# Partition sums of the key norm and the group norm from two float32r parts

## The chip, the core and the metric

The kernel runs on one core of one Trainium2 chip, in one launch. The metric is the device time of an execution in microseconds (us). A core has a matrix engine (TensorE, PE in the profile, with its weight loads shown as PEld), a vector engine (VectorE, DVE), a scalar engine (ScalarE, ACT), GpSimd (POOL) and SyncE (SP), which issues most transfers. Each runs its own queue of instructions in order, and they wait for each other by semaphores. Products accumulate in PSUM, which ACT and DVE read.

## The reference

Two transformer layers on 256 tokens of width 2048, in float32. The first layer has three branches (a banded attention A, an RWKV-7 time mix B and an attention C over a memory of 256 tokens), the second another three and a feed-forward part. Most of the work is products of the activations with weights. The change lies in branch B, whose 16 heads of 64 are handled here in eight pairs:

```python
def rwkv7_time_mix(...):
    ...
    kk = heads(k * f(k_k))
    kk = kk * lax.rsqrt(jnp.maximum(jnp.sum(kk * kk, axis=-1, keepdims=True), 1e-24))
    k = k * (1.0 + (a - 1.0) * f(k_a))
    ...
    o = rwkv7_scan(rh, dh, kh, vh, -kk, kk * ah)
    mean = jnp.mean(o, axis=-1, keepdims=True)
    var = jnp.mean(jnp.square(o - mean), axis=-1, keepdims=True)
    o = ((o - mean) * lax.rsqrt(var + GN_EPS)).reshape(bsz, s, B_WIDTH) * f(ln_w) + f(ln_b)
    bonus = jnp.sum(rh * kh * f(r_k), axis=-1, keepdims=True) * vh
    return o + bonus.reshape(bsz, s, B_WIDTH)
```

The sum of squares in `kk` is the key norm; `mean` and `var` are the group norm. All three sum over a head's 64 channels.

## The kernel before

Activations are kept with channels on the 128 partitions and the 256 tokens along the free dimension, so a tile of 128x256 holds a pair of heads. A sum over a head's channels is then a sum over partitions; it is made on PE, as a product with the constant `bdones` (two 64x64 blocks of ones on the diagonal, part of the constant tile `con`), and comes out on every partition of the head.

**Products of the weights.** A float32 weight is split into two float32r parts: `wh`, rounded by ACT (line 171), and the rest `wl`, by DVE (line 179) or GpSimd (line 177); the activations lie ready split in `xg`. `gemm_B` (line 182) gives a 128x256 tile by pairs of products, one of 512 columns with `wh` and one of 256 with `wl`; `gemm_A` (line 208) fills two PSUM tiles at once. Their PSUM tiles are named g and come from a pool of three banks (line 117). `evict` (line 218) adds the two halves of a g tile up: ACT copies one to `et`, DVE adds the other.

**Branch B, per pair p.** `rwkv_inputs(p)` (line 528) projects k, r and v. Each projection is evicted into a tile `zr`, of which there are two (line 494), and `shift` (line 429) mixes it with its neighbour token: an ACT multiplication into tile `tA` and a DVE step. Then come the decay, the key norm (lines 557 to 564: square, sum into `pk`, maximum, `rsqrt`, multiplication), the bonus sum and the operands `atrt`, `bt_d`, `kt_d` and `v_d`. `rwkv_inverse(p)` (line 584) inverts a triangular matrix per head and chunk, in five levels of small products (tiles Z and D on PE, Z and tt on DVE). `rwkv_chain(p)` (line 652) goes through four chunks of 64 tokens one after the other (products ch and oT on PE, copies X, U and S on DVE) and ends with the group norm in lines 687 to 698, the chain's tail here. Working tiles of branch B come from `tmp(tag)` (line 523), most with one buffer a tag: a tile takes the buffer over when the last reader of the tile ahead of it in the program is done.

**Order.** The program text issues chain(p), inverse(p + 1), inputs(p + 2) and then fillers: gate projections, products of branch A and merge gates (lines 780 to 823). A scheduler sets each engine's queue from that text by times of its own, within the limits of data and buffers. Two fillers hold PSUM for long: A0 (after the first pair) is copied out into `r16b`, whose memory the keys and values `mkv` of attention C hold until its last head is done, and A1 (after the fifth) overwrites queries that attention A still reads.

Of the kernel before, what the change touches and what calls it, by code (L numbers as in the profile page):

```python
# [100 lines left out]
def _body(tc, a, out):  # L101
    nc = tc.nc
# [26 lines left out]
    def P(n, j=0, w=1):  # L129
        o, _ = _P[n]  # L130
        return par[:, o + j:o + j + w]
# [208 lines left out]
    if True:  # L340
# [182 lines left out]
        def tmp(tag, bufs=1, shape=(128, 256), dt=F32):  # L523
            return rw.tile(list(shape), dt, tag=tag, name=tag, bufs=bufs)

        pair = {}

        def rwkv_inputs(p):

            k = tmp("k")  # L530
            shift(k, raw_tile(gemm_B(a["w1B"][1 + p], xg)), P("mu_k", p), 8 + p)
            r = tmp("r")
            shift(r, raw_tile(gemm_B(a["w1B"][9 + p], xg)), P("mu_r", p), p)
            v = tmp("v")
            shift(v, raw_tile(gemm_B(a["w1B"][17 + p], xg)), P("mu_v", p), 16 + p)
            w2 = tmp("t0")
            nc.sync.dma_start(w2, a["lora2"][p])
            pl = ps_small("pl")
            mm(pl[:, 0:256], w2[:, 0:128], lora)
            mm(pl[:, 256:512], w2[:, 128:256], lora)  # L540
            s = tmp("s")
            nc.scalar.activation(s, pl[:, 0:256], AF.Tanh, bias=hw0[:, p:p + 1], scale=0.5)
            av_ = tmp("a")
            nc.scalar.activation(av_, pl[:, 256:512], AF.Tanh, bias=hw0[:, 8 + p:9 + p], scale=0.5)
            nc.scalar.activation(s, s, AF.Copy, bias=0.5, scale=0.5)
            nc.scalar.activation(av_, av_, AF.Copy, bias=0.5, scale=0.5)
            cum = tmp("cum")
            nc.vector.tensor_tensor_scan(cum, C("scan"), s, 0.0, op0=ALU.mult, op1=ALU.add)
            nc.gpsimd.tensor_sub(s, cum, s)
            e1 = s  # L550
            nc.scalar.activation(e1, s, AF.Exp, scale=-DECAY_C)
            ep = tmp("ep", 2)
            nc.scalar.activation(ep, cum, AF.Exp, scale=-DECAY_C)
            en = cum
            nc.scalar.activation(en, cum, AF.Exp, scale=DECAY_C)

            kk = tmp("kk")
            t0 = tmp("t0")
            nc.scalar.activation(t0, k, AF.Square, scale=P("k_k", p))
            pk = ps_small("pk")  # L560
            mm(pk[:, 0:256], bdones, t0)
            nc.vector.tensor_scalar(t0, pk[:, 0:256], 1e-24, None, op0=ALU.max)
            rsqrt(t0, tmp("tA"))
            nc.vector.scalar_tensor_tensor(kk, k, P("k_k", p), t0, op0=ALU.mult, op1=ALU.mult)

            nc.scalar.activation(t0, av_, AF.Identity, bias=om[:, 25 + p:26 + p], scale=P("k_a", p))
            nc.vector.tensor_mul(k, t0, k)

            nc.vector.scalar_tensor_tensor(t0, r, P("r_k", p), k, op0=ALU.mult, op1=ALU.mult)
            mm(pk[:, 256:512], bdones, t0)  # L570
            nc.vector.tensor_mul(raw[:, 8 + p, :], v, pk[:, 256:512])

            atrt = atrt_b[p % 2]
            diag(atrt, 64, lambda d, sl: nc.vector.scalar_tensor_tensor(
                d, c4(kk)[sl], -1.0, c4(e1)[sl], op0=ALU.mult, op1=ALU.mult))
            nc.vector.tensor_mul(atrt[:, :, 0:64], c4(r), c4(ep))
            nc.gpsimd.tensor_mul(kk, kk, av_)
            diag(bt_d, 0, lambda d, sl: nc.vector.tensor_mul(d, c4(kk)[sl], c4(en)[sl]))
            diag(kt_d, 0, lambda d, sl: nc.vector.tensor_mul(d, c4(k)[sl], c4(en)[sl]))
            diag(v_d, 0, lambda d, sl: nc.gpsimd.tensor_copy(d, c4(v)[sl]))  # L580

            pair[p] = dict(atrt=atrt, ep=ep)
# [69 lines left out]
        def rwkv_chain(p):  # L652

            d = pair.pop(p)
            atrt, ep, tok = d["atrt"], d["ep"], d["tok"]
            po = ps_small("oT", "o")
            S = None
            for c in range(4):
                gm, tf = d["gm"][c // 2][:, c % 2], d["tf"][c // 2][:, c % 2]
                pc = ps_small("ch", "c")  # L660
                if S is not None:
                    mm(pc[:, 0:128], atrt[:, c, 64:192], S, start=True, stop=False)
                mm(pc[:, 0:128], gm[:, 64:192], tok[:, 2, c], start=S is None, stop=True)
                x_ = tmp("X", 1, (128, 128))
                nc.vector.tensor_copy(x_, pc[:, 0:128])
                mm(pc[:, 128:256], tf, x_)
                u_ = tmp("U", 1, (128, 128))
                nc.vector.tensor_copy(u_, pc[:, 128:256])
                if c < 3:
                    mm(pc[:, 256:384], tok[:, 1, c], tok[:, 2, c], start=True, stop=False)  # L670
                    mm(pc[:, 256:384], tok[:, 0, c], u_, start=False, stop=True)
                    sn = tmp("S", 2, (128, 128))
                    dc = ep[:, c * 64 + 63:c * 64 + 64]
                    if S is None:
                        nc.vector.tensor_scalar(sn, pc[:, 256:384], dc, None, op0=ALU.mult)
                    else:
                        sd = tmp("Sd", 1, (128, 128))
                        nc.gpsimd.tensor_scalar(sd, S, dc, None, op0=ALU.mult)
                        nc.vector.scalar_tensor_tensor(sn, pc[:, 256:384], dc, sd, op0=ALU.mult, op1=ALU.add)
                o_ = po[:, c * 64:(c + 1) * 64]  # L680
                if S is not None:
                    mm(o_, S, atrt[:, c, 0:64], start=True, stop=False)
                mm(o_, tok[:, 2, c], gm[:, 0:64], start=S is None, stop=False)
                mm(o_, u_, gm[:, 192:256], start=False, stop=True)
                if c < 3:
                    S = sn
            oT = tmp("oT", 1)
            nc.scalar.copy(oT, po[:, 0:256])

            mm(po[:, 256:512], bdones, oT)  # L690
            nc.vector.scalar_tensor_tensor(oT, po[:, 256:512], -1.0 / 64, oT, op0=ALU.mult, op1=ALU.add)
            q_ = tmp("gq")
            nc.scalar.activation(q_, oT, AF.Square)
            mm(po[:, 0:256], bdones, q_)
            nc.vector.tensor_scalar(q_, po[:, 0:256], 1.0 / 64, GN_EPS, op0=ALU.mult, op1=ALU.add)
            rsqrt(q_, tmp("gy"))
            nc.vector.scalar_tensor_tensor(oT, oT, P("ln_w", p), q_, op0=ALU.mult, op1=ALU.mult)
            nc.vector.scalar_tensor_tensor(raw[:, 8 + p, :], oT, P("ln_b", p), raw[:, 8 + p, :], op0=ALU.add, op1=ALU.add)
# [451 lines left out]
```

## Time and profile before

| | us |
|---|---|
| median of three timed runs | 2940.38 |
| lowest, highest | 2939.12, 2940.76 |
| the profiled execution | 2939.36 |
| its span, first to last instruction | 2937.5 |
| PE, DVE, ACT, GpSimd busy in the span | 2910.8, 1867.4, 1471.0, 573.5 |

The span is 1.86 us shorter than the time of the same execution. Branch B with its fillers runs from about 100 to 880 us; then come the merge, the output product and the second layer. Busy time is the time in which an engine executes instructions; a PE that is busy need not run at its peak, since the ends of its products are modelled. A row of the timeline gives the start, the duration, the engine, the line, the operation, the tile written and those read, how many instructions are merged into it, and in brackets how long the engine had been idle before it and what ended the wait. All products show line 150 or 153, those of the helpers `tr` and `mm`, so they are told apart by their tiles.

### The profile page before, as it was taken

The numbers are of one execution on the slowest core, as the hardware profiler recorded it, in microseconds if no ns is written. First come the engines' busy times: TensorE is split into PE (matmuls) and PEld (weight loads), VectorE is DVE, ScalarE is ACT, GpSimd is POOL, SyncE is SP. The second block draws the span as 40 slices with busy tenths as digits, with TensorE's granted clock in tenths as the row PEclk, the third lists the DMA queues.
The fourth block names the chain that finished last, engine by engine and source line by source line (L and its number), as shares of the span: only waits on it lengthen the run. The fifth ranks groups of instructions, "written<-read, shape, count | busy, mean of one in ns | idle before, by whom it ended". The sixth has DMA issues, their size and how long they took to land.

```text
span 2937.5 us, 44420 instructions
## 1 busy us (share of the span) xinstructions
PE 2910.8 (99%) x16696; PEld 2562.2 (87%) x16696; DVE 1867.4 (64%) x3040; ACT 1471.0 (50%) x2249; POOL 573.5 (20%) x806
## 2 busy tenths in 40 slices
PE   9999999999999999999999999999999999999998
PEld 7888888888988888888888888888888888888887
DVE  7455675567647655657667766666666666666554
ACT  7544455455456554545544454444555444444443
POOL 0676576566652000000000000000000000000000
PEclk9999999999999999999999999999999999999999
DMA  7554344444357555655455555555555555555654
GB/s 287 188 168 131 118 134 138 135 135 133 127 173 239 195 188 197 209 177 174 148 173 172 188 192 188 192 187 193 187 187 194 187 193 188 192 188 189 191 187 150
DMA packets 150535, 522.44 MB, mean 178 GB/s; under 512 B 17120, under 2 KB 22624, under 8 KB 150320
## 3 DMA queue, kind: packets, MB, share of 16 engines
q1 hardware_dynamic: 148064, 513.61, 53.2%
q0 software_dynamic: 1824, 4.98, 0.5%
q8 instruction: 131, 2.15, 0.3%
q10 hardware_dynamic: 432, 1.02, 0.1%
q14 instruction: 84, 0.69, 0.1%
HBM read 514.56 MB, written 4.98 MB: 177 GB/s over the span
## 4 chain that ended last, share of the span: by engine, by line
PE 95%; DVE 3%; ACT 1%; POOL 1%; issue 0%; DMA 0%; DVEq 0%; SPq 0%; ACTq 0%
PE g L153 88%; PE D L153 1%; PE ch L153 1%; PE G L153 1%; PE Z L153 1%; PE oT L153 1%; PE sc L153 1%; PE po L153 1%; POOL wl L177 0%; PE ptk L150 0%; DVE wl L179 0%; PE glo L153 0%; ACT wh L171 0%; PE pt L150 0%; DVE yhl L235 0%
## 5 line engine op out<-in xcount | busy, mean ns | idle before, releaser
L153 PE MATMUL g<-xg,wh 128*128 128x512 f32 x4640 | 1631.4, 392 | 1.2 <-DVE zr L223 1.2
L171 ACT CAST wh<-w 128x1024 fp32r<-128x1024 f32 (+1 forms) x962 | 1001.8, 1042 | 1218.4 <-PE g L153 702.7
L179 DVE TENSOR_TENSOR wl<-w,wh 128x1024 fp32r<-128x1024 f32 (+1 forms) x809 | 986.7, 1220 | 727.4 <-ACT wh L171 722.4
L153 PE MATMUL g<-xg,wl 128*128 128x256 f32 x4640 | 1319.4, 284 | 1.4 <-DVE wl L179 1.4
L153 PEld LDWEIGHTS g<-xg,wh 128*128 128x128 f32 x4640 | 870.3, 188 | 178.1 <-DVE zr L223 1.3
L153 PEld LDWEIGHTS g<-xg,wl 128*128 128x128 f32 x4640 | 875.6, 189 | 3.8 <-DVE wl L179 2.0
L177 POOL TENSOR_TENSOR wl<-w,wh 128x256 fp32r<-128x256 f32 x612 | 463.5, 790 | 202.8 <-ACT wh L171 177.8
L153 PE MATMUL g<-yhl,wh 128*128 128x512 f32 x768 | 269.6, 390 | 0.0
L153 PE MATMUL g<-wh,xg 128*128 128x512 f32 x768 | 246.3, 402 | 0.4 <-ACT va L356 0.4
L153 PE MATMUL g<-act,wh 128*128 128x512 f32 x704 | 244.2, 390 | 0.0
L153 PE MATMUL g<-yhl,wl 128*128 128x256 f32 x768 | 216.6, 282 | 0.0
L153 PE MATMUL g<-act,wl 128*128 128x256 f32 x704 | 198.7, 282 | 0.0
L851 POOL TENSOR_TENSOR accm<-accm,z 128x256 f32<-128x256 f32 x64 | 53.4, 834 | 651.3 <-DVE z L850 651.3
L153 PEld LDWEIGHTS g<-yhl,wh 128*128 128x128 f32 x768 | 144.2, 188 | 30.3
L153 PEld LDWEIGHTS g<-wh,xg 128*128 128x128 f32 x768 | 143.3, 188 | 31.1 <-ACT va L356 0.5
L220 ACT COPY et<-g 128x256 f32<-128x256 f32 (+1 forms) x433 | 156.9, 362 | 1.1 <-PE g L153 1.1
L153 PEld LDWEIGHTS g<-act,wh 128*128 128x128 f32 x704 | 132.2, 188 | 27.7
L153 PE MATMUL g<-wl,xg 128*128 128x512 f32 x384 | 149.5, 403 | 0.0
L153 PEld LDWEIGHTS g<-yhl,wl 128*128 128x128 f32 x768 | 145.2, 189 | 0.0
L153 PEld LDWEIGHTS g<-act,wl 128*128 128x128 f32 x704 | 133.1, 189 | 0.0
L223 DVE TENSOR_TENSOR z<-g,et 128x256 f32<-128x256 f32 x215 | 89.9, 418 | 17.9 <-ACT et L220 17.5
L153 PE MATMUL g<-mg,wh 128*128 128x512 f32 x256 | 88.7, 390 | 0.0
(369 smaller groups left out, 2771.1 us busy)
## 6 DMA issues: line engine op xcount, KB each, us to landing
w<-w2B SPq DMA_DIRECT2D x208, 512.0 KB, 3.3
w<-w1B SPq DMA_DIRECT2D x194, 512.0 KB, 3.3
w<-w_gate SPq DMA_DIRECT2D x88, 512.0 KB, 3.4
w<-w_ffup SPq DMA_DIRECT2D x88, 512.0 KB, 3.3
w<-w1A SPq DMA_DIRECT2D x64, 512.0 KB, 3.3
w<-w_down SPq DMA_DIRECT2D x64, 448.0 KB, 3.3
w<-w_o SPq DMA_DIRECT2D x32, 512.0 KB, 3.4
w<-w2A SPq DMA_DIRECT2D x32, 512.0 KB, 3.3
```

Source lines behind the costliest of these rows:

```text
L153: nc.tensor.matmul(dst, lhsT=lhsT, rhs=rhs, start=start, stop=stop)
L171: nc.scalar.copy(wh[:, :nel], w[:, :nel])
L177: nc.gpsimd.tensor_sub(wl[:, sl], w[:, sl], wh[:, sl].bitcast(F32))
L179: nc.vector.tensor_sub(wl[:, :nel], w[:, :nel], wh[:, :nel].bitcast(F32))
L220: nc.scalar.copy(t[:m], ps[:m, 256:512])
L223: nc.vector.tensor_add(z[:m], ps[:m, 0:256], t[:m])
L851: nc.gpsimd.tensor_add(accm, accm, u)
```

## The change

The three sums are taken of two float32r parts with a float32r copy of the ones matrix. The value is rounded to float32r by ACT (`hi`), DVE subtracts that from the value (`lo`), and both are multiplied with `bd_r` into the same PSUM tile. The bonus sum stays as it is. The parts need buffers and take tags that exist: for the key norm `tA` (also of `shift` and `rsqrt`) and `kk`, for the first group norm sum `gy` and `a` (the tag of the learning rate in `rwkv_inputs`), for the second `gy` and `tA`; the square `q_` goes from a tag of its own to `a`. The tile `kk` is allocated after the sum.

```diff
         pair = {}
+        bd_r = rw.tile([128, 128], F32R, tag="bdr", name="bd_r")
+        nc.vector.tensor_copy(bd_r, bdones)
+
+        def head_sums(dst, src, hi, lo):
+
+            nc.scalar.copy(hi, src)
+            nc.vector.tensor_sub(lo, src, hi.bitcast(F32))
+            mm(dst, bd_r, hi, start=True, stop=False)
+            mm(dst, bd_r, lo, start=False, stop=True)
...
-            kk = tmp("kk")
             t0 = tmp("t0")
             nc.scalar.activation(t0, k, AF.Square, scale=P("k_k", p))
             pk = ps_small("pk")
-            mm(pk[:, 0:256], bdones, t0)
+            head_sums(pk[:, 0:256], t0, tmp("tA", dt=F32R), tmp("kk", dt=F32R))
             nc.vector.tensor_scalar(t0, pk[:, 0:256], 1e-24, None, op0=ALU.max)
             rsqrt(t0, tmp("tA"))
+            kk = tmp("kk")
...
-            mm(po[:, 256:512], bdones, oT)
+            head_sums(po[:, 256:512], oT, tmp("gy", dt=F32R), tmp("a", dt=F32R))
             nc.vector.scalar_tensor_tensor(oT, po[:, 256:512], -1.0 / 64, oT, op0=ALU.mult, op1=ALU.add)
-            q_ = tmp("gq")
+            q_ = tmp("a")
             nc.scalar.activation(q_, oT, AF.Square)
-            mm(po[:, 0:256], bdones, q_)
+            head_sums(po[:, 0:256], q_, tmp("gy", dt=F32R), tmp("tA", dt=F32R))
```

The scheduler orders the queues anew. The numbers behind names below tell tiles of one name apart and differ between the two kernels; lines of the changed kernel from 527 on are 9 or 10 higher.

ACT, around the first pair's tail. Before: the key norm's rsqrt of the second pair, then the first `shift` of the third pair (it reads the projection k in zr_2728), 24 rows ahead of the tail's first copy:

```order
L256 ACT_TABLE_LOAD
L256 ACTIVATE tA_2078<-t0_2073 128x256
L432 ACTIVATE tA_2733<-zr_2728,om_911 128x256
L171 CAST wh_3025<-w_3023 128x1024
L566 ACTIVATE t0_2073<-a_2061,om_911,par_91 128x256
L171 CAST wh_3046<-w_3044 128x1024
L432 ACTIVATE tA_2793<-zr_2788,om_911 128x256
L432 ACTIVATE tA_2850<-zr_2845,om_911 128x256
```

The same engine now, where line 697 is the tail's first copy, line 532 the rounding of a high part, and tA_2755 the third pair's first shift:

```order
L697 COPY oT_2388<-oT_2329 128x256
L532 CAST gy_2390<-oT_2388 128x256
L485 COPY pT_2449<-pt_2442 128x512
L702 ACTIVATE a_2397<-oT_2388 128x256
L532 CAST gy_2399<-a_2397 128x256
L432 ACTIVATE tA_2755<-zr_2750,om_911 128x256
L256 ACT_TABLE_LOAD
L256 ACTIVATE gy_2406<-a_2397 128x256
L432 ACTIVATE tA_2815<-zr_2810,om_911 128x256
L432 ACTIVATE tA_2872<-zr_2867,om_911 128x256
```

The third pair's shifts have moved from ahead of the tail to behind its last rounding.

PE, at the end of the filler A0 (its two PSUM tiles are g_2898 and g_2899). Before, the gate product g_3067 follows at once, and goes on between products of the chain:

```order
L153 MATMUL g_2899<-wh_3046,xg_110 128x512 x2
L153 MATMUL g_2899<-wl_3048,xg_110 128x512
L153 MATMUL g_3067<-xg_110,wh_3070 128x512
L153 MATMUL g_3067<-xg_110,wl_3072 128x256
L153 MATMUL g_3067<-xg_110,wh_3070 128x512
L153 MATMUL g_3067<-xg_110,wl_3072 128x256
L153 MATMUL sc_2406<-kT_2392,qT_2391 128x256
L153 MATMUL ch_2331<-S_2327,atrt0_977 128x128
```

The same place now, where A0 has g_2925 and g_2926:

```order
L153 MATMUL g_2926<-wh_3073,xg_110 128x512 x2
L153 MATMUL g_2926<-wl_3075,xg_110 128x512
L153 MATMUL ch_2330<-btok_976 128x128
L153 MATMUL ch_2330<-U_2335,btok_976 128x128
L153 MATMUL oT_2329<-gm_1549,U_2335 128x64
L153 MATMUL pk_2081<-t0_2079,con_92 128x256
L153 MATMUL ch_2343<-S_2339,atrt0_977 128x128
L153 MATMUL ch_2343<-btok_976,gm_1549 128x128
```

The gate product, now g_3094, comes 98 rows further on, behind the tail's second sum and the fifth level of the second pair's inverse (its last D tile):

```order
L153 MATMUL D_2664<-tt_2502,Z_2657 128x128
L153 MATMUL D_2670<-Z_2662,tt_2525 128x128
L153 MATMUL D_2670<-tt_2525,Z_2662 128x128
L153 MATMUL D_2670<-Z_2662,tt_2525 128x128
L153 MATMUL D_2670<-tt_2525,Z_2662 128x128
L153 MATMUL g_3094<-xg_110,wh_3097 128x512
L153 MATMUL g_3094<-xg_110,wl_3099 128x256
```

PE has moved all products of weights out of the rows in between. It has done so a second time, in the sixth pair's chain (oT_5743), behind the last product of A1 (g_6248); 73 rows follow without a g tile:

```order
L153 MATMUL g_6248<-wh_6395,xg_110 128x512 x2
L153 MATMUL g_6248<-wl_6397,xg_110 128x512
L153 MATMUL ch_5774<-S_5767,atrt0_977 128x128
L153 MATMUL ch_5774<-btok_976,gm_4827 128x128
L153 MATMUL oT_5743<-atrt0_977,S_5767 128x64
L153 MATMUL oT_5743<-gm_4827,btok_976 128x64
L153 MATMUL Z_5891<-tt_5827,lmr_5846 128x128 x2
L153 MATMUL Z_5896<-tt_5850,lmr_5869 128x128 x2
```

Before, weight products stood between the steps of that chain too, as they did in the first.

## Rows read from the trace of the kernel before

**Rows 1.** The page, busy us (share of the span) and instructions by engine.

```profile
PE 2910.8 (99%) x16696; PEld 2562.2 (87%) x16696; DVE 1867.4 (64%) x3040; ACT 1471.0 (50%) x2249; POOL 573.5 (20%) x806
```

**Rows 2.** Stretches: length, busy us (instructions) of PE, PEld, DVE, ACT, POOL; clock, DMA, GB/s.

```profile
265.00:300.00 35.00, 34.64 (x208) 30.65 (x206) 28.45 (x60) 14.14 (x24) 20.80 (x29) 1.00 0.37 114
300.00:330.00 30.00, 28.39 (x176) 25.38 (x176) 15.83 (x32) 11.88 (x18) 12.04 (x17) 1.00 0.32 108
...
2920.00:2930.00 10.00, 4.37 (x24) 3.30 (x22) 3.97 (x8) 1.77 (x4) 0.00 (x0) 0.91 0.00 0
```

**Rows 3.** PE's waits, 100 to 880 us: total us, times, longest us.

```profile
PE g L153 <- DVE zr L223: 1.2, 1, 1.2
...
PE ch L153 <- DVE U L668: 0.2, 1, 0.2
```

**Rows 4.** Tiles pk and oT: passes, ns min/median/max, first and last start.

```profile
L153 PE MATMUL pk<-t,con x32: 377/379/432, 129.3 to 673.6; 128*128 128x256 f32 x32
...
L153 PE MATMUL oT<-oT,con x16: 377/379/483, 309.1 to 859.3; 128*128 128x256 f32 x16
...
L153 PE MATMUL oT<-gq,con x16: 377/379/382, 313.7 to 864.2; 128*128 128x256 f32 x16
```

**Rows 5.** The chain of waits in order of time: start, us, what.

```profile
233.66 1.73 PE sc L153 x8
```

**Rows 6.** Timeline of PE, 311 to 313 us.

```profile
311.43 0.28 PE L153 MATMUL g<-xg,wl 128*128 128x256 f32 x1
311.55 0.39 PE L153 MATMUL g<-xg,wh 128*128 128x512 f32 x1
...
312.88 0.27 PE L153 MATMUL D<-tt,Z 128*128 128x128 f32 x1
312.99 0.27 PE L153 MATMUL D<-Z,tt 128*128 128x128 f32 x1
```

**Rows 7.** Groups by form, 240 to 880 us: count, busy us, mean ns, idle before.

```profile
L606 ACT CAST lmr<-lt 128x256 fp32r<-128x256 f32 x14 | 5.7, 405 | 13.7 <-DVE lt L602 13.6
...
L626 DVE TENSOR_TENSOR Z<-Z,msk 128x256 fp32r<-128x256 f32 x70 | 27.7, 417 | 14.8 <-PE Z L153 14.4
```

**Rows 8.** Timeline, tails of the first and the last chain.

```profile
309.11 0.30 PEld L153 LDWEIGHTS oT<-oT,con 128*128 128x128 f32 x2 [0.23 <-ACT oT L688]
...
314.92 1.28 ACT L256 ACT_TABLE_LOAD   x1
...
855.36 0.37 ACT L688 COPY oT<-oT 128x256 f32<-128x256 f32 x1 [0.85 <-PE oT L153]
...
859.05 0.59 PE L153 MATMUL oT<-oT,con 128*128 128x256 f32 x2
```

**Rows 9.** Timeline, shift of the third pair, gate product, tail, copy of A0.

```profile
262.30 0.51 ACT L432 ACTIVATE tA<-zr,om 128x256 f32<-128x256 f32 x1 [2.87 <-DVE t L262]
...
269.47 0.52 DVE L433 SCALAR_TENSOR_TENSOR k<-zr,par,tA 128x256 f32<-128x256 f32 x1
270.03 0.43 DVE L223 TENSOR_TENSOR zr<-g,et 128x256 f32<-128x256 f32 x1
...
274.60 0.39 PE L153 MATMUL g<-xg,wh 128*128 128x512 f32 x1
...
313.73 0.59 PE L153 MATMUL oT<-gq,con 128*128 128x256 f32 x2
...
327.72 1.08 ACT L354 COPY r16b<-g 128x512 f32<-128x512 f32 x2
```

**Rows 10.** Timeline of DVE, 433 to 434 us.

```profile
433.28 0.41 DVE L600 TENSOR_TENSOR tt<-G,msk 128x256 fp32r<-128x256 f32 x1
433.61 0.41 DVE L601 TENSOR_TENSOR gm<-G,msk 128x256 f32<-128x256 f32 x1
```

**Rows 11.** Timeline of PE, 5 to 22 us.

```profile
6.36 2.08 PE L153 MATMUL g<-wh,mem_hl 128*128 128x512 f32 x4 [6.36 <-ACT wh L166]
...
10.80 1.10 PE L153 MATMUL g<-wh,mem_hl 128*128 128x512 f32 x4
```

## The prediction

> **What bounds the kernel now.** I read the busy line of the page first: TensorE (PE) is busy for 99% of the span, and VectorE (DVE) and ScalarE (ACT) for 64% and 50% [rows 1]. Then the table of stretches around the first head pair's chain: PE is busy in 34.64 of 35.00 us and in 28.39 of 30.00 us, while DVE has 28.45 and 15.83 [rows 2]. Then the list of PE's waits from 100 to 880 us, which holds the whole changed code: eight entries, the first 1.2 us and the last 0.2 us, some 4 us in all [rows 3]. So PE's own work sets the time, and two things can move it: less PE work, or an order in which PE has nothing to run. The page's profiled execution took 2939.36 us, 1.86 us more than its span, and 1.0 us less than the median of the three timed runs (2940.38); I work out a difference and add it to the median.
>
> **What the change saves.** There are 24 changed sums: one key norm and two group norm sums in each of eight passes. Each shows as two passes of 128x256: 16 instructions a line in the group norm, and in the key norm 16 of the 32 on tile pk, the other 16 being the bonus sum, which stays float32 [rows 4]. A run of eight such passes takes 1.73 us, 0.216 us each [rows 5], so a sum costs 0.43 us. A float32r product of 256 columns is followed by the next after 0.12 us [rows 6]; two make 0.24 us. The saving is 24 x 0.19 = 4.6 us of PE, all on the path. Where it stands alone the time is 2935.8.
>
> **What it adds beside PE.** 24 rounding copies on ACT, near the 405 ns of a copy of that shape, and 24 subtractions on DVE, near the 417 ns of a tensor op of that shape that writes float32r [rows 7], so 10 us on each. They lie beside products of the weights as long as PE has any. Each sum then comes some 0.9 us later (0.40 + 0.42 and two handovers). The cover for that is the lead that the order leaves: in the last chain the copy ends at 855.36 + 0.37 = 855.73 and the sum starts at 859.05, 3.3 us later [rows 8]. In the first chain there is no lead, and PE's weight load waited 0.23 us [rows 8]. I cost the later arrival at nothing where weight products run; with no lead anywhere it would be 24 x 0.4 = 10 us for the second part's wait behind the first. The one-off copy of the ones matrix is a single DVE instruction and costs nothing.
>
> **What it moves, and what that costs.** The new parts live in buffers that others use. The second group norm sum of a chain keeps its low part in tag tA, of which there is one, and the next user of tA is the token shift of the pair two ahead. In the order of before that shift stands 24 ACT rows ahead of the chain's tail, now it stands right behind the tail's last rounding. The rows of before show what hangs on it, for the first chain: the shift's ACT half ran at 262.30, the k shift at 269.47, and the third projection could then be added up out of PSUM at 270.03, which freed its bank, so that the next product (moving operand wh, a gate) began at 274.60; the chain's second sum came only at 313.73 [rows 9]. The other two of the three g banks hold projection A0, whose copies out run at 327.72 [rows 9], since they write over the memory keys that the last attention there still reads. So with the shift behind the tail all three banks are held, and no product of weights can run until the chain has ended. The order of the changed kernel shows just that: 126 small products of the chain, the next inverse and two attention heads between the last product of A0 and the first of the gate, with not one weight product among them. In the order of before gate and later products are spread through the same work.
>
> How long does this take? PE's part, priced from rows: 13 float32 products of 256 columns at 0.43 = 5.6; 60 float32r products of 128 columns at the 0.11 between two of tile D [rows 6] = 6.6; 12 transposes, one pass each, at 0.11 = 1.3; 19 float32 products of 128 columns at half of 0.43 = 4.1; 8 of 192 at 0.32 = 2.6; 14 of 64 at about 0.2 = 2.8. Together 23 us. DVE has 74 instructions between its first (the chain's U) and the one that frees the bank (the third zr). In the stretch of before that runs the same work, 60 took 28.45 us, 0.474 each [rows 2], so 74 take 35.1 us. That is the upper end: 12 us over PE. But an instruction of 0.41 us can start 0.33 us after the one ahead [rows 10], which takes 0.08 x 74 = 5.9 us off: 29.2. Allow DVE a lead of 3 us from the products ahead of the stretch, and the lower end is 29.2 - 3 - 23 = 3 us. I take 29.2 plus some 2 us in which DVE itself waits for PE or ACT, less 23: **8 us**. It is nearer to the spacing than to the durations, because most of these are independent.
>
> It happens a second time, at the sixth chain, where A1 holds two banks until two attention heads have read what it overwrites. There the order has 92 small products without a weight product (56 float32r at 0.11, ten transposes at 0.11, and 26 others for 5.4: 12.7 us) against 40 DVE instructions: 19.0 us by 0.474, 15.8 by the spacing. DVE's last step there, the one that frees the bank, stands behind the norm's first multiplication, which waits for the rsqrt and its table load of 1.28 us [rows 8]. The ends are 1 us (15.8 less a lead of 2 less 12.7) and 9 us (19.0 plus 2.5 of waits less 12.7); I take **5.5 us**. In the other chains A projections leave their banks at once, two banks rotate, and I cost the coupling at nothing: their order keeps weight products between the steps.
>
> The sum: -4.6 + 8 + 5.5 = +8.9 us, so 2948.3 for a run like the profiled one and **2949** on the median.
>
> **The rivals.** *DVE keeps up.* If its instructions in the two stretches take no longer than PE's, which needs 23/74 = 0.31 us each in the first, only the saving is left: 2940.4 - 4.6 = 2935.8, not slower than before. For it: many of them start 0.33 us apart, and GpSimd, which was busy in 20.80 of 35.00 us [rows 2], will have little to do there. Against: every inverse level has steps that depend on each other across DVE and PE, and DVE was already at 28.45 of 35.00 us with weight products to spare. *The lower ends.* Stalls of 3 and 1 us give 2939.8, and anything under 10.5 us in all stays within 0.2% (5.9 us, about what a measurement of this kernel can tell from no change). *The clock falls, or more waits appear.* In 2920 to 2930 us, with PE busy for 4.37 us, the granted clock was 0.91 [rows 2], so between its two levels of 1.2 and 2.4 GHz; and after the idle start four products of 512 columns took 2.08 us where four a little later took 1.10 [rows 11], though the record there says 1.00. If both stretches ended at the low level, some 2 to 3 us of slowed products would follow each, and with the stalls at their upper ends (12 + 9) the time is 2940.4 - 4.6 + 21 + 5 = 2961.8. Missing leads at the sums would end there too. The Trainium skill, "TensorE: Matmul & The Clock Gate", Part 1, says that the array's default is the throttled 1.2 GHz and that activity releases it; by that rule the stretches would be followed by slow products and the time would be the 2954 of 2949 + 5. The trace's start agrees with it; no row of before shows a stretch as thinly filled as these, so I keep it as part of this rival.
>
> **How the numbers follow.** Forecast (both stretches stall, 10.5 us or more in all): 0.55, 2949. Lower ends: 0.22, about 2941. DVE keeps up: 0.12, 2935.8. Clock or more waits: 0.11, about 2960. The first and the last are slower by over 0.2%, less a little for the forecast's edge: slower 0.62. Within 0.2%: the lower ends and nearly all of the second rival, 0.34. Faster by over 0.2% needs more than the whole saving: 0.04. The range leaves out half of the keeping-up case below and half of the worst case above: 2936 to 2960.
>
> **What would show it.** Right: PE idle of 5 to 12 us in all between the last product of A0 and the gate's first, some 260 to 305 us into the span, with waits on DVE's Z, tt, X and zr; a second such place near 570 to 600 us; DVE busy there for nearly all of it; products pk and oT with con replaced by pairs of 0.12 us. Wrong: PE as full there as in [rows 2], or the stall elsewhere, or waits of PE on the sums' low parts, which I cost at nothing. What I know least is how closely DVE's instructions follow each other in those stretches.

## The result, and the profile after

The changed kernel takes 2960.32 us (median of four runs, 2959.4 to 2963.4) against 2940.57 for the kernel before: a ratio of 1.0070, with a 95% interval from 1.0058 to 1.0083. It is slower by 19.8 us where 8.9 were forecast, and its profiled execution (2960.94 us, span 2959.2) is 21.7 us longer in span than that of before.

The page's busy line answers to [rows 1]. PE is busy for 9.7 us longer, though it has less work; the rest of the 21.7 us is idle PE:

```profile
PE 2920.5 (99%) x16696; PEld 2567.1 (87%) x16696; DVE 1877.5 (63%) x3065; ACT 1492.0 (50%) x2280; POOL 578.6 (20%) x806
```

The sums themselves are as forecast: in the tile list of pk the float32 passes have halved ([rows 4]: 32, the bonus sum's 16 are left), and 16 passes of 0.28 us have come in.

```profile
L153 PE MATMUL pk<-t,con x16: 377/379/483, 143.2 to 757.5; 128*128 128x256 f32 x16
L153 PE MATMUL pk<-tA,bd_r x8: 279/280/582, 133.2 to 744.5; 128*128 128x256 f32 x8
L153 PE MATMUL pk<-kk,bd_r x8: 279/284/522, 133.5 to 745.0; 128*128 128x256 f32 x8
```

The stretches show where the time went (length, busy us and instructions of PE, PEld, DVE, ACT, POOL, granted clock, DMA share, GB/s). The first two answer to [rows 2]:

```profile
265.00:300.00 35.00, 31.22 (x198) 27.53 (x197) 29.66 (x78) 10.65 (x21) 11.41 (x15) 1.00 0.25 79
300.00:330.00 30.00, 29.62 (x178) 26.36 (x177) 18.83 (x39) 19.78 (x34) 14.73 (x23) 1.00 0.29 93
398.00:402.00 4.00, 1.53 (x9) 1.16 (x9) 3.96 (x4) 1.14 (x3) 3.19 (x6) 0.89 0.66 185
402.00:408.00 6.00, 6.00 (x22) 5.22 (x22) 4.67 (x9) 4.02 (x6) 5.03 (x9) 0.50 0.41 155
600.00:606.00 6.00, 5.10 (x32) 4.00 (x31) 5.81 (x20) 2.70 (x9) 0.00 (x0) 1.00 0.07 22
606.00:616.00 10.00, 9.26 (x32) 8.01 (x32) 6.28 (x16) 4.06 (x7) 0.29 (x3) 0.50 0.01 2
```

In 265 to 300 us, the first stretch without weight products, PE was idle for 3.8 us of 35 (0.4 before). In 606 to 616 us, behind the second stretch, the granted clock was 0.50, the lower of its two levels (1.2 GHz), for 10 us; and the same for 6 us behind a wait near 400 us that no step of the prediction has. Before, no stretch from 100 to 900 us is below 1.00.

The hold itself is as forecast. The timeline of the changed kernel that answers to [rows 9] (start, us, engine, line, operation, tiles, count, idle before and releaser):

```profile
273.43 0.40 PE L153 MATMUL g<-wl,xg 128*128 128x512 f32 x1
...
300.02 0.34 PE L153 MATMUL oT<-tA,bd_r 128*128 128x256 f32 x1
...
300.40 0.51 ACT L432 ACTIVATE tA<-zr,om 128x256 f32<-128x256 f32 x1 [0.94 <-PE oT L153]
301.37 0.47 DVE L433 SCALAR_TENSOR_TENSOR k<-zr,par,tA 128x256 f32<-128x256 f32 x1
302.43 0.41 DVE L223 TENSOR_TENSOR zr<-g,et 128x256 f32<-128x256 f32 x1
...
304.18 0.45 PE L153 MATMUL g<-xg,wh 128*128 128x512 f32 x1
```

The second sum's low part leaves tA, the shift of the third pair takes it (ACT waited for PE), the k shift frees a zr, the third projection leaves its bank, and the gate product begins: 304.18 instead of 274.60. The first line shown is A0's last weight product. The second place looks alike; here are A1's last weight product and the next one:

```profile
591.90 0.40 PE L153 MATMUL g<-wl,xg 128*128 128x512 f32 x1
...
610.07 0.80 PE L153 MATMUL g<-xg,wh 128*128 128x512 f32 x1 [0.74 <-DVE zr L223]
```

From the end of the one to the start of the other the two stretches are these (columns as above):

```profile
273.83:304.18 30.35, 26.19 (x177) 23.37 (x176) 26.55 (x74) 10.16 (x21) 6.86 (x10) 1.00 0.13 40
592.30:610.07 17.77, 16.13 (x111) 14.55 (x109) 14.70 (x41) 7.57 (x16) 2.89 (x5) 0.88 0.21 67
```

They last 30.4 and 17.8 us, where the prediction's terms make 31.2 (29.2 and 2) and 18.2 (12.7 and 5.5). DVE has 74 and 41 instructions in them, where 74 and 40 were counted. PE was idle for 4.2 and 1.6 us; the rest of what it lost there is products that stand further apart.

PE's waits from 100 to 880 us (us in total, times, longest) answer to [rows 3]. There are 18 entries now, and the longest is new:

```profile
PE pk L153 <- ACT tA L532: 2.5, 1, 2.5
PE po L153 <- ACT pT L733: 1.5, 1, 1.5
...
PE oT L153 <- DVE a L533: 0.2, 1, 0.2
...
```

The last line shown is all that PE waited for a group norm's low part.

**How much, and where.** A busy PE need not run at its peak, so I worked out a lost time: the length of a stretch less what its products take at the spacings of the kernel before. The spacings come from a fit over the 78 stretches of 10 us between 100 and 880 us of that trace (0.235 us for a weight product of 512 columns, 0.115 for 256, 0.113 for a float32r one of 128, 0.225 for a float32 pass of 256, and so on; a float32r one of 256 taken as 0.12). The time at a low clock is one less the granted clock, summed over stretches of 5 us, and it is part of the lost time.

| us lost by PE | before | after |
|---|---|---|
| 260 to 380 | 4.4 | 6.7 |
| 380 to 440 | 0.2 | 5.5 |
| 440 to 560 | -1.7 | 1.1 |
| 560 to 660 | -1.3 | 10.6 |
| all of 100 to 940 | 1.8 | 27.4 |
| of it at the lower clock | 0.0 | 8.5 |

25.6 us more are lost, and the sums save some 5: that is near the 20, but the total is not to be leaned on. With one spacing for all products of 128 columns the same fit gives 22.3 in place of 27.4, while a place moves by 1 to 2 us. (For the other kernels the lost time comes out 1 to 6 us above what their medians say; I use it to tell places apart, not for totals.) The two places of the forecast hold 2.3 and 11.9 of it; 5.3 come near 400 us, and the rest is spread. Of the 11.9 no more than some 8.4 belong to the second stretch, since waits of 0.90 us at 574.52, 1.10 at 622.64 and 1.47 at 630.26 lie outside it. What was lost at the lower clock is an upper bound of what the clock cost.

### The profile page after: what moved, and what is told of

Read it like the earlier page. It is cut to its first block, busy times and chain, and to the rows that moved or that the text cites. A ratio compares the mean times of both kernels' runs of the same rounds, so it can differ in the third digit from the quotient of the medians.

```text
span 2959.2 us, 44486 instructions
## 1 busy us (share of the span) xinstructions
PE 2920.5 (99%) x16696; PEld 2567.1 (87%) x16696; DVE 1877.5 (63%) x3065; ACT 1492.0 (50%) x2280; POOL 578.6 (20%) x806
## 4 chain that ended last, share of the span: by engine, by line
PE 77%; DVE 1%; ACT 0%; issue 0%; DVEq 0%
PE g L153 74%; PE ch L153 0%; PE po L153 0%; PE sc L153 0%; PE glo L153 0%; PE D L153 0%; PE G L153 0%; PE oT L153 0%; DVE yhl L235 0%; PE kv L153 0%; PE Z L153 0%; PE pt L150 0%; PE ptk L150 0%; DVE wl L179 0%; PE gln L153 0%
## 5 line engine op out<-in xcount | busy, mean ns | idle before, releaser
L223 DVE TENSOR_TENSOR z<-g,et 128x256 f32<-128x256 f32 x215 | 89.8, 418 | 25.6 <-ACT et L220 25.1
```

The costliest lines, as they stand in the source:

```text
L223: nc.vector.tensor_add(z[:m], ps[:m, 0:256], t[:m])
```

## What happened near 400 us

The timeline of the changed kernel around its longest wait, in four engines:

```profile
397.50 3.13 DVE L707 SCALAR_TENSOR_TENSOR raw<-oT,par,raw 128x256 f32<-128x256 f32 x1
397.56 2.78 POOL L177 TENSOR_TENSOR wl<-w,wh 128x256 fp32r<-128x256 f32 x4
...
400.55 0.47 DVE L433 SCALAR_TENSOR_TENSOR v<-zr,par,tA 128x256 f32<-128x256 f32 x1
401.06 0.41 ACT L532 CAST tA<-t 128x256 fp32r<-128x256 f32 x1 [2.86 <-DVE v L433]
401.52 0.58 PE L153 MATMUL pk<-tA,bd_r 128*128 128x256 f32 x1 [2.47 <-ACT tA L532]
...
402.97 0.63 PE L153 MATMUL g<-xg,wh 128*128 128x512 f32 x1
...
403.61 0.63 PE L153 MATMUL g<-xg,wh 128*128 128x512 f32 x1
```

Read it from the bottom. Pairs of weight products stand 0.64 us apart where 0.35 is usual: the clock is low. PE had waited 2.47 us for the key norm's high part; ACT could not round it, since tag tA was still read by the shift of v; and that shift stood on DVE behind a step of the chain's tail which took 3.13 us, against 0.47 of the same line at 479.01, while GpSimd made four subtractions in a row. In the kernel before the key norm needs tA only behind its sum, for `rsqrt`, and from 100 to 900 us no single 128x256 step of DVE takes over 1.3 us. The Trainium skill, "SBUF — State Buffer", "SBUF: two separate sides", says that a DVE step with two inputs in SBUF and a GpSimd step shut each other out for a whole instruction. The trace agrees in kind, but here DVE waited for four.

The key norm's part is what waited here, and not what makes the place. In 380 to 440 us PE's listed waits come to 2.7 us in the changed kernel, 3.0 in e2 (no key norm part in tA), 2.2 in e4 (no parts at all) and 2.8 in e9, and to 1.1 us at most in every other kernel here. These four have a group norm tile in tA and two zr tiles; e12, with a third zr, has none of these waits. The longest entry of the list in e2, e4 and e9, one line each:

```profile
PE D L153 <- DVE Z L635: 3.0, 1, 3.0
```

```profile
PE Z L153 <- DVE tt L634: 2.2, 2, 1.2
```

```profile
PE D L153 <- DVE Z L635: 1.8, 1, 1.8
```

So it is a third stall of the coupling through tA, at the second pair's tail.

## What tag a holds

The prediction speaks of tA alone. The other tag that the change shares, `a`, turned out as dear by itself (e10 below). The square `q_` now lies in it, and the learning rate of the pair two ahead, which takes the same tag, is read out of PSUM tile pl (two products with `lora`, lines 551 and 553 of the changed kernel). The timeline of the changed kernel for one such pair:

```profile
437.44 1.03 PE L153 MATMUL pl<-lora,t 128*128 128x256 f32 x4
...
439.89 0.47 ACT L551 ACTIVATE s<-pl,hw 128x256 f32<-128x256 f32 x1
...
478.28 0.47 DVE L706 SCALAR_TENSOR_TENSOR oT<-oT,par,a 128x256 f32<-128x256 f32 x1
...
480.10 0.48 ACT L553 ACTIVATE a<-pl,hw 128x256 f32<-128x256 f32 x1
```

The first half of pl is read at once; the second waits 40 us, until the chain's tail has read `a` for the last time (line 706). All that time pl keeps its PSUM bank, the only one of the pool that also serves the scores, transposes and outputs of attention A. It happens for four pairs (358.97 to 397.27, 437.44 to 480.10, 511.32 to 559.96, 712.27 to 743.80). In kernel e11 below, which has the whole change but for the group norm's tags, the same two steps are 1.4 us apart:

```profile
414.14 1.03 PE L153 MATMUL pl<-lora,t 128*128 128x256 f32 x4
...
415.58 0.46 ACT L553 ACTIVATE a<-pl,hw 128x256 f32<-128x256 f32 x1
```

## The experiments

Ratios are to the kernel before, run beside each (medians 2940.61, 2940.34 and 2940.16 us in the three groups of four). Lost time as above, from the profiled execution, which in e2, e9 and e10 lies 1.5 to 3 us above the median; the kernel before loses 1.8 us.

| kernel | median us | ratio, 95% interval | PE lost | at the lower clock |
|---|---|---|---|---|
| after | 2960.32 | 1.0070 (1.0058 to 1.0083) | 27.4 | 8.5 |
| e1 | 2966.59 | 1.0090 (1.0076 to 1.0104) | 34.0 | 11.9 |
| e2 | 2963.90 | 1.0073 (1.0059 to 1.0087) | 35.0 | 18.8 |
| e3 | 2952.46 | 1.0041 (1.0029 to 1.0054) | 21.6 | 5.1 |
| e4 | 2957.68 | 1.0067 (1.0054 to 1.0080) | 22.5 | 3.4 |
| e5 | 2941.49 | 1.0004 (0.9995 to 1.0012) | 7.7 | 0.0 |
| e6 | 2935.15 | 0.9982 (0.9973 to 0.9991) | 2.7 | 0.0 |
| e7 | 2941.19 | 1.0004 (0.9995 to 1.0012) | 7.7 | 0.0 |
| e8 | 2937.82 | 0.9992 (0.9983 to 1.0001) | 5.3 | 0.0 |
| e9 | 2968.63 | 1.0100 (1.0086 to 1.0113) | 39.6 | 17.1 |
| e10 | 2974.81 | 1.0116 (1.0101 to 1.0132) | 47.3 | 20.5 |
| e11 | 2935.70 | 0.9986 (0.9977 to 0.9995) | 4.7 | 0.0 |
| e12 | 2962.00 | 1.0075 (1.0062 to 1.0088) | 29.4 | 13.7 |

**e1: the second low part out of tA.** It goes to the buffer of `rs_bc`, which nothing uses between the first normalisation and the second layer.

```diff
-            head_sums(po[:, 0:256], q_, tmp("gy", dt=F32R), tmp("tA", dt=F32R))
+            head_sums(po[:, 0:256], q_, tmp("gy", dt=F32R), const.tile([128, 256], F32R, tag="rsbc", name="gl"))
```

> The changed kernel, but the low part of the second group norm sum has a buffer of its own in place of tag tA. Theory A (the shift of the pair two ahead waits for that part in tA, and the weight products stop in two stretches): in the order the first stretch without a weight product shrinks from 22.4 to 6.6 us of PE work and the second goes to another place with 6.6. In the trace of the changed kernel PE loses some 7 us in 260 to 320 us and some 10 us in 600 to 640 us, 5 of them at a granted clock of 0.50. So A expects 2960 - 17 = 2943, 2941 to 2947, with the wait at the key norm's first part near 399 us (2.5 us and half the clock for 6.6 us after it) perhaps still there. Theory B (the later arrival of the 24 sums, the added copies and subtractions cost it, wherever the parts lie): 2958 to 2961. Theory C (the key norm's part in tA is the main cause): 2958 to 2961 too.

2966.59: slower still, and outside the ranges of all three theories. The first stretch is mended in part (3.3 us lost in 260 to 300 against 6.2), but 23.8 us are lost in 560 to 660. So tA is not the whole cause, as I had it; with tag `a` still shared, taking tA's part out gained nothing.

**e2: the key norm's high part out of tA.**

```diff
-            head_sums(pk[:, 0:256], t0, tmp("tA", dt=F32R), tmp("kk", dt=F32R))
+            head_sums(pk[:, 0:256], t0, const.tile([128, 256], F32R, tag="rsbc", name="kh"), tmp("kk", dt=F32R))
```

> The changed kernel, but the high part of the key norm has a buffer of its own in place of tag tA, so that its rounding need not wait for the shift of v. The two stretches without weight products stay in the order (22.4 and 10.9 us of PE work). Theory A: the wait near 399 us and the half clock after it go (2.5 + 3.4 us), so 2954, 2951 to 2957, with PE still losing 7 us in 260 to 320 us and 5 to 10 us near 600 us. Theory B: 2958 to 2961. Theory C: 2943 or less.

2963.90, outside all three ranges again. The wait for tA at 400 us is gone, but a step of DVE (line 706) is held for 3.46 us beside GpSimd at 404.94, PE waits 3.0 us for another tile, and the clock falls all the same. It also falls behind the first stretch here (10 us of lost time at the lower clock in 280 to 320), where it did not in the changed kernel.

**e3: all parts in other buffers**, the key norm's high part in that of `rs_bc`, both low parts of the group norm and its square in the ring `sq` of three tiles.

```diff
...
-            head_sums(po[:, 256:512], oT, tmp("gy", dt=F32R), tmp("a", dt=F32R))
+            head_sums(po[:, 256:512], oT, tmp("gy", dt=F32R), scr.tile([128, 256], F32R, tag="sq", name="gl", bufs=3))
...
-            q_ = tmp("a")
+            q_ = scr.tile([128, 256], F32, tag="sq", name="gq", bufs=3)
...
```

> The changed kernel with no shared tag: key norm's high part, both low parts of the group norm and its square have buffers of their own; the sums are still float32r. Theory A: only the saving of 24 x 0.19 = 4.6 us is left, 2936, 2934 to 2939, below the kernel before. Theory B: 2950 or more, since every sum still comes 0.9 us later and the 48 added instructions are all there.

2952.46, which by the numbers written down speaks for theory B and against A. It is faster than the changed kernel, e1 and e2, but 12 us slower than before, and half of its loss lies at the end of branch B: PE waits 4.4 us at 898.89 for a head of attention A, and 10.7 us are lost in 880 to 940. The order showed why the heads come late: the norms of attention A take a tile of the same ring, and in the order of this kernel the first head's scores stand behind a tail. That `sq` was the reason is argued from the order; e8 leaves the group norm out of that ring and has the heads where they were.

**e4: the coupling through tA alone**, in the kernel before, with float32 sums.

```diff
-            mm(po[:, 0:256], bdones, q_)
+            q2 = tmp("tA")
+            nc.scalar.copy(q2, q_)
+            mm(po[:, 0:256], bdones, q2)
```

> The kernel before, all sums float32 as there, but the square of the group norm is copied by ACT into a tile of tag tA, and the second sum is taken of that copy: 8 added copies, and the coupling alone. In the order two stretches without weight products appear, of 20.6 and 14.6 us of PE work. Theory A: PE loses as much there as in the changed kernel, 7 us at the first, 5 to 10 at the second, so 2940.5 + 12 to 17 = 2952 to 2958. Theory B: 2940 to 2942, since no float32r part and no subtraction is there.

2957.68: one tag in eight places costs 17 us with no float32r part anywhere. It lies at the upper end of the range given, and two of its five executions lie above it (2961.71 and 2965.93).

**e5: the control to e4**, the same copy into a buffer that nothing uses.

```diff
-            q2 = tmp("tA")
+            q2 = const.tile([128, 256], F32, tag="rsbc", name="gl")
```

> The control to e4: the kernel before, all sums float32, the square of the group norm copied by ACT as in e4, but into a buffer that nothing else uses. In the order the attention heads of A and the chains stand where the kernel before has them, and there is no stretch without weight products of over 4.1 us. Theory A, wider now (it is the shared buffers, whichever they are: each makes work of another pair, or of attention A, wait for a chain's tail, and PE then runs out of covered work): 2940 to 2942. Theory D (any edit, even a neutral one, makes the scheduler lay the work out anew, and the layout of before is a lucky one): 2945 to 2965.

2941.49, no different from before. So the 16 us between e4 and e5 are the tag, not the eight copies, and a neutral edit does not lay the work out badly. Theory D falls.

**e6 and e7: the group norm alone, the key norm alone**, with buffers that hold up nothing (the room comes from a single buffer for a small tile of the head norms, `part`). In e6 the key norm is that of before; in e7 the group norm is.

```diff
+            head_sums(po[:, 256:512], oT, tmp("gy", dt=F32R), const.tile([128, 256], F32R, tag="rsbc", name="gl"))
...
+            q_ = tmp("gq")
...
+            head_sums(po[:, 0:256], q_, tmp("gy", dt=F32R), const.tile([128, 256], F32R, tag="rsbc", name="gl"))
```

> The changed kernel with the group norm's 16 sums alone in float32r parts; the key norm is that of before. The low parts have a buffer that nothing else uses, the square its own tag as before. Theory A: only the saving of 16 x 0.19 = 3.1 us, 2937.5 (2936 to 2940). Theory B (the later arrival and the added instructions cost it): 2943 or more, two thirds of e3's 2952. Theory D: 2945 to 2965.

> The kernel before with the key norm's 8 sums alone in float32r parts, the high one in tag kk, the low one in a buffer that nothing else uses. Theory A: the saving of 8 x 0.19 = 1.5 us, 2939 (2937 to 2941). Theory B: 2943. Theory D: 2945 to 2965.

e6 takes 2935.15, 5.2 us less than before and a little better than the 3.1 of the sum; e7 2941.19, no different from before, where 1.5 us less were worked out. e6 is far from theory B; e7 lies between A's 2939 and B's 2943 and does not tell them apart.

**e8: all 24 sums with free buffers**: e6, and the key norm's parts in `kk` and in the ring `sq`.

```diff
+            head_sums(pk[:, 0:256], t0, tmp("kk", dt=F32R), scr.tile([128, 256], F32R, tag="sq", name="kl", bufs=3))
```

> All 24 sums in float32r parts, as in the changed kernel, but no buffer that holds up other work: key norm in kk and a ring that is idle then, group norm in gy and a buffer that nothing else uses, the square in its own tag as before. It differs from e3, where three tiles of the chain's tail shared the ring from which the norms of attention A take a tile; in the order of e3 the first head of attention A stood 41 us of weight products later than before, here it stands where it stood. Theory A: 2936 (2934 to 2939), the fastest of all. Theory B: 2945 or more, as in e3. Theory D: 2945 to 2965.

2937.82, in theory A's range, though not the fastest, which is e6. All 48 added instructions and the later arrival of every sum are in it, and it loses 3.5 us more than before, none of it at a low clock. Theory B falls.

**e9, e10, e11: one shared buffer at a time, put back into e8.**

```diff
 e9:
-            head_sums(po[:, 0:256], q_, tmp("gy", dt=F32R), const.tile([128, 256], F32R, tag="rsbc", name="gl"))
+            head_sums(po[:, 0:256], q_, tmp("gy", dt=F32R), tmp("tA", dt=F32R))
 e10:
-            head_sums(po[:, 256:512], oT, tmp("gy", dt=F32R), const.tile([128, 256], F32R, tag="rsbc", name="gl"))
-            q_ = tmp("gq")
+            head_sums(po[:, 256:512], oT, tmp("gy", dt=F32R), tmp("a", dt=F32R))
+            q_ = tmp("a")
 e11:
-            head_sums(pk[:, 0:256], t0, tmp("kk", dt=F32R), scr.tile([128, 256], F32R, tag="sq", name="kl", bufs=3))
+            head_sums(pk[:, 0:256], t0, tmp("tA", dt=F32R), tmp("kk", dt=F32R))
```

> e8 with one of the three shared buffers put back: the low part of the second group norm sum in tag tA, as in the changed kernel. The order has the changed kernel's two stretches again (22.4 and 12.9 us of PE work without a weight product). Theory A by the losses read from the trace of the changed kernel (some 5 us in 260 to 320, 4 near 400, 10 in 600 to 640 with half of it at a granted clock of 0.50): 2938 + 12 to 20 = 2950 to 2958. If this one buffer is all of it, it equals the changed kernel, 2959 to 2961. Rival (the tag of the square and of the first low part, a, carries it): 2938 to 2942.

> e8 with the first low part and the square of the group norm in tag a, as in the changed kernel; the learning rate of the pair two ahead then waits for the tail. In the order it stands as e1 does (second stretch of 6.6 us, first head of attention A 43 us of weight products later than before). Theory A, in its wider form: as slow as e1, 2958 to 2967, since PE would lose most in 560 to 660 us. Rival (tA alone carries it, and e1 was slow for the key norm's part in tA): 2938 to 2942.

> e8 with the key norm's high part in tag tA and the low one in kk, as in the changed kernel. In the order every sum and head stands within a few us of e8's place. Theory A: the rounding waits for the shift of v, which has mostly run by then: 2937 to 2941. Rival (this is what makes e1 and the changed kernel slow): 2945 or more.

e9 is 31 us slower than e8, e10 37 us, e11 2 us faster (and just below its range). So each of the two group norm tags is by itself enough, and the key norm's part in tA is harmless. Both sizes were forecast too small, and the two do not add up: with both, and the key norm's part in tA, the changed kernel is faster than either.

The stretches of e9 around the first one, which answer to [rows 2] in smaller steps (columns as above). PE is short of work from 275 us on, and at 292 us the clock falls for some 20 us:

```profile
275.00:280.00 5.00, 3.79 (x23) 2.99 (x21) 3.34 (x9) 0.57 (x1) 5.00 (x7) 1.00 0.40 131
...
285.00:290.00 5.00, 4.00 (x26) 3.53 (x25) 4.89 (x17) 1.68 (x6) 1.20 (x1) 1.00 0.00 0
290.00:295.00 5.00, 4.66 (x29) 4.45 (x28) 4.07 (x12) 0.25 (x1) 0.00 (x0) 0.68 0.00 0
295.00:300.00 5.00, 5.00 (x27) 5.00 (x25) 2.62 (x6) 0.71 (x2) 0.00 (x0) 0.50 0.00 0
```

The busy share of PE rises where the clock falls: a chain product that takes longer looks busier.

In e10 the loss is elsewhere. Its stretches:

```profile
265.00:300.00 35.00, 33.24 (x201) 29.51 (x199) 27.30 (x68) 15.01 (x26) 16.92 (x26) 1.00 0.33 109
...
560.00:600.00 40.00, 34.90 (x187) 30.88 (x186) 31.39 (x75) 17.81 (x28) 17.90 (x26) 0.83 0.30 100
600.00:660.00 60.00, 51.16 (x280) 44.24 (x279) 26.97 (x68) 18.86 (x35) 17.98 (x25) 0.88 0.24 78
```

and its timeline of PE where it waits longest, at a head of attention A:

```profile
643.03 0.34 PE L153 MATMUL Z<-Z,tt 128*128 128x128 f32 x2
647.68 0.55 PE L150 MATMUL pt<-con,tp 128*128 128x128 f32 x3 [4.32 <-DVE tp L727]
648.86 1.65 PE L153 MATMUL po<-pT,raw 128*128 128x256 f32 x4 [0.62 <-ACT pT L733]
651.02 1.11 PE L150 MATMUL tra<-con,r16b 128*128 128x128 f32 x4 [0.51 <-DVE raw L784]
```

Here a head's transposes, its output product and the next head's transposes stand on PE with no weight product between them, so PE waits out the softmax. That the bank held by pl brought the heads there is argued from the times; no run gives pl a bank of its own. The list of the products that give a head's output shows the heads' place (first and last start) in before, after and e10, one line each:

```profile
L153 PE MATMUL po<-pT,raw x32: 272/350/432, 528.9 to 807.8; 128*128 128x256 f32 x16, 128*128 128x128 f32 x16
```

```profile
L153 PE MATMUL po<-pT,raw x32: 272/378/634, 594.8 to 863.9; 128*128 128x256 f32 x16, 128*128 128x128 f32 x16
```

```profile
L153 PE MATMUL po<-pT,raw x32: 272/377/796, 604.7 to 885.3; 128*128 128x256 f32 x16, 128*128 128x128 f32 x16
```

In e11 they run from 526.7 to 813.4, as before. But in e9 and e4, with tA alone, they start late too (598.7 and 591.1), so the heads' place alone is not the mark of tag `a`. The page and the stretches of e11, to be set beside those of after:

```profile
PE 2905.9 (99%) x16696; PEld 2558.3 (87%) x16696; DVE 1870.1 (64%) x3065; ACT 1479.0 (50%) x2271; POOL 573.4 (20%) x806
```

```profile
265.00:300.00 35.00, 32.67 (x197) 28.88 (x195) 28.04 (x69) 15.02 (x26) 16.01 (x24) 1.00 0.32 109
...
560.00:600.00 40.00, 40.00 (x239) 35.44 (x238) 24.22 (x62) 18.58 (x31) 24.36 (x33) 1.00 0.42 139
600.00:660.00 60.00, 59.70 (x357) 52.05 (x357) 43.74 (x84) 31.55 (x52) 35.71 (x50) 1.00 0.45 143
```

PE's busy time is 4.9 us below [rows 1], against the 4.6 of the sum.

**e12: one link of the chain of holds undone**, a third `zr` tile in the changed kernel (with single buffers for two small tiles, `part` and `sm`).

```diff
-            z = rw.tile([128, 257], F32, tag="zr", name="zr", bufs=2)
+            z = rw.tile([128, 257], F32, tag="zr", name="zr", bufs=3)
```

> The changed kernel with all its shared buffers, but three zr tiles in place of two (room for it comes from single buffers for two small tiles of the attention). It undoes one link of the chain of holds: a projection can be added up out of its bank though the shift behind it waits for tA. In the order the two long stretches are gone (7.6 us is the longest). Theory A with the link at zr: PE loses under 3 us in 260 to 310 us where the changed kernel loses 6, and nothing at the sixth chain's tail; the tag a is still shared, so the heads of attention A still come late, and the time is between e10's and e8's, 2945 to 2962. Rival (the stretches come from elsewhere, as from the banks that A0 and A1 hold): the same losses and 2958 to 2961.

2962.00, no gain, at the upper edge of what I gave and 1 us above the rival's range, so the time does not choose between them. The stretches of e12:

```profile
265.00:300.00 35.00, 33.89 (x209) 30.45 (x207) 28.74 (x68) 13.62 (x23) 17.15 (x22) 1.00 0.37 124
300.00:330.00 30.00, 29.01 (x173) 25.50 (x173) 19.23 (x43) 13.42 (x23) 9.51 (x16) 0.94 0.25 75
```

PE has 33.89 us in 265 to 300 where the changed kernel has 31.22, and its gate product follows A0 at 272.89 instead of 304.18, so `zr` is the link by which tA stops the weight products there. But 4.3 us go in 300 to 320, 1.7 of them to the clock, and others at later places (at 618 us, by the sixth tail, the clock fell, where nothing was to be lost), so the time does not come back: undoing one link moves the waits.

**Against both kernels.** e6 and e11 are faster than the kernel before, by intervals that leave out 1, and by some 25 us faster than the changed one. e11 is the changed kernel with the group norm's parts and square moved out of `a` and `tA`, and `part` with one buffer, so its 24.6 us over the changed kernel are what the group norm's shared buffers cost there. (`part` alone has no run; e7 has it too and is no faster than before.)

## Why the prediction was wrong, point by point

- **The saving, 24 x 0.19 = 4.6 us on PE's path: right.** e11 is 4.5 us faster than before, e8 2.5. By parts it is less even: the group norm gave 5.2 for 3.1, the key norm -0.9 for 1.5, which cannot be told from nothing.
- **ACT's and DVE's added work, and the later arrival of the sums, at nothing: right to some 2 us.** e8 holds all of it and falls 2.1 us short of the saving, e11 0.1; PE waited for a low part of the group norm 0.2 us in the changed kernel.
- **The two stretches: the place, the mechanism and the length right, the loss too large.** The order's two stretches lost time, e9 brings them back with tA alone, and e12 shows the zr link. They last 30.4 and 17.8 us for 31.2 and 18.2. I gave 8 and 5.5 us of loss. The first lost 5.2 us more than before in 260 to 320, of which 2.9 are made good by 380, since the kernel before loses there; PE's idle time in it, 4.2 us, is a little under the 5 that I had named as the sign. The second lost 8.4 at most, of which up to 5.1 are the clock. So some 8.5 us without the clock stand against 13.5, and these two terms are not what made the forecast too low.
- **"In the other chains ... I cost the coupling at nothing": wrong, the first step that failed.** Some 12 of the 25.6 us lie outside the two stretches, 5.3 of them near 400 us at the second pair's tail (3.4 of these at the lower clock). I had followed tag tA into the first and the sixth chain alone, and tag `a`, which the same diff shares, nowhere. For four pairs the second half of pl waited 31 to 49 us for the tail, and a PSUM bank with it. Over e8, tA alone costs 31 us (e9) and `a` alone 37 (e10). How the changed kernel's loss divides between the two no run says: without tA's part it is 6 us slower (e1), without either 24.6 faster (e11). The key norm's part in tA, which I did not price either, is harmless by e11.
- **The clock: no term in the sum, the second step that failed.** I gave 2 to 3 us behind each stretch, worked out from no row, and only in a rival at 0.11. The fall behind the second stretch cost up to 5.1 us, the one near 400 us 3.4, and behind the first there was none: 8.5 in all. With the 8.6 us that were lost elsewhere at the full clock this is 17 us that the sum had at nothing, and the stalls priced too high take back 5. (The 0.91 that I read as a clock between its two levels is a mean: in that trace the clock is 1.00 up to 2928.2 us and 0.50 behind.) The rival named the time almost exactly (2961.8 for 2960.3), though its working took both stalls at their upper ends, which they did not reach: that was luck.
- **DVE keeps up, and the lower ends: out.** DVE was busy for 29.66 of 35 us in the first stretch, as worked out, and PE lost more than the 4 us of the lower ends.
- **What stays open.** Much the same first stretch of products ends at the full clock in the changed kernel and in e4, and at the half clock in e2 and e9. Part of this changes from one execution of a kernel to the next: three of e4's five took 2957.2 to 2957.7 us at a mean granted clock of 0.997, the others 2961.7 at 0.995 and 2965.9 at 0.993, and e2's five range from 2955.9 at 0.997 to 2966.7 at 0.992. So the order of a kernel does not settle whether the clock falls, and executions of one kernel that differ in the clock differ by 9 to 11 us. And the tags' costs do not add up: 31 and 37 alone, 22 together with the key norm's over e8. I have no number that foretells either.

## What to carry to other kernels

When an edit takes an existing buffer for a new tile, list every other user of that buffer, and for each what it holds while it waits (a PSUM bank, a second buffer, a place in a queue); here the diff's cost lay there and not in its instructions. Price each such wait by a neutral control, the same edit with a buffer that nothing uses, before pricing the arithmetic. And where PE is the bound, a place in which it runs short of products can cost twice: the gap, and the slower clock that may follow, in some executions and not in others.

## What the runs showed of the hardware that was not expected

- The granted clock fell to 0.50 at 606 us in the changed kernel with no long wait of PE ahead of it: PE was busy in 5.10 of the 6 us before, and its longest listed wait there was 0.41 us. The Trainium skill, "TensorE: Matmul & The Clock Gate", "Why this matters for your kernels", tells one to avoid long idle gaps between bursts; by that alone the clock would have stayed up here, so the trace does not agree that long gaps are all that brings it down. A single wait of 2.47 us near 400 us was followed by a fall too, and waits of 1.47 and 1.58 us in e3 (276.72 and 361.69 us) were not.
- A DVE step of 128x256 that takes 0.42 us, or 0.96 beside one subtraction of GpSimd (396.28), took 3.13 us beside four (397.50), and 3.05 at 699.09; in e10 one took 6.09 us at 769.33, beside eight. There was none over 1.3 in the kernel before, from the same number of GpSimd instructions; which steps are caught differs from order to order, and I have no rule for it.
